# Weight sums held back by marks, attention in whole-chunk steps, and the last norm in blocks: a two-layer hybrid decoder on one core

## The chip, the cores and the metric

The kernel runs on one core of one Trainium2 chip. A core has five engines that run their own instruction queues and wait for each other by semaphores: TensorE (PE; its weight loads are shown as PEld), VectorE (DVE), ScalarE (ACT), GpSimd (POOL) and SyncE (SP). SP, ACT and POOL also issue DMAs, which 16 DMA engines carry out. The metric is the device time of one execution in microseconds (us), the median of several runs. "Line" numbers (L187) are those of the kernel before.

## The reference

Two layers over x of 512 rows by 2048. A layer projects its input to 16 heads in three groups: six forgetting-attention heads ("fox", causal attention with a cumulative log-forget bias), six sparse-attention heads ("dsa", rotary; an indexer with 16 small heads picks 128 keys per query) and four heads that read 256 memory rows. Every head is multiplied by a SiLU gate, all heads go through one output projection, and x becomes LayerNorm(alpha * x + y). All values are float32.

```
h = x @ w_in                       # q, k, v, gate of every group, forget logits, indexer
fox: softmax(q.k * scale + c_q - c_k, causal) @ v,  c = cumsum(log_sigmoid(f_logit + b_forget))
dsa: keys = top_k(sum_h relu(q_idx.k_idx) * w_idx);  softmax(q.k * scale over keys) @ v
mem: softmax(q.k_mem * scale) @ v_mem,  (k_mem, v_mem) = mem @ w_mem_kv
y = concat(fox, dsa, mem) * silu(gates) @ w_out
x = layer_norm(alpha * x + y) * ln_gain + ln_bias
```

## The kernel before

The work is a stream of weight chunks of 1 MB (128 x 2048, `raw`). `load_w` has SP load a chunk two chunks ahead into one of three buffers; `split_w` splits each half of it, three halves ahead of its use, into a high part on ScalarE (`whi`, L180) and the rest on VectorE (`wlo`, L181). `product` makes one float32 product out of three matmuls (L187 to L189). A layer's chunks are, in order: the memory's values (`mv`, 4) and keys (`mk`, 4), the queries and gates of the memory heads (`mq`, `mg`, 4 pairs), one chunk of small columns, eight for the indexer's queries (`iq`), and then for every four heads four chunks of values (`val`) followed by gate, query and key of each head (`fg`, `fq`, `fk` or `dg`, `dq`, `dk`). A chunk of queries is 48 matmuls of 128x512.

The output projection (`out`) is a seven-product matrix scheme, 14 steps of two chunks (`OUT_ORDER`), 24 matmuls of 128x512 a chunk. It needs sums of weight blocks, T1 to T4. `weight_sums` makes them in DRAM: 32 DMAs of 1 MB a layer, all issued by POOL, half of them plain copies (L307) and half adds into memory (L304).

What isn't matmuls of the stream is written as generators. `begin` puts one on a list and `tick` advances each by a step; `tick` runs after the first half of a chunk and at its end, so the order in the code is fixed by hand. `attend` is one fox or dsa head: scores (`s`, L530), softmax (`pr`), transposes of the probabilities (`pt`, L560) and the product with the values (`po`), each of them a step or two after the other. For a fox head `forget_bias` loads a row of forget sums (`ck`, POOL's queue) and lets POOL make the bias tiles (`bt`). `late_operands` splits the left operands of the output projection. The tiles of 128x512 come from one pool of 69 buffers (`slot`), the accumulators from 8 banks (`bank`); a new tile waits until its buffer's last readers are done.

At the end of layer 1 the rows are normalised in four blocks of 128 rows (`finish`). Blocks 2 and 3 are complete after step ("Q5", 1), six chunks before the end; blocks 0 and 1 with the last chunk. `finish` treats the first 512 columns on ScalarE and POOL (L713 to L715, output DMA on ScalarE's queue) and the other three on VectorE in two passes (L718, L721, output DMA on SP's queue).

Of the kernel before, what the change touches and what calls it, by code (L numbers as in the profile page):

```python
# [139 lines left out]
def kernel(  # L140
# [147 lines left out]

    where = {c: i for i, c in enumerate(all_chunks())}

    def weight_sums(l):

        every = [(pair, g) for pair in range(2) for g in range(2)]
        for name, first, second in (("T1", (0, 0), (0, 1)), ("T3", (0, 1), (1, 1)),
                                    ("T2", "T1", (1, 1)), ("T4", "T2", (1, 0))):
            for step in (first, second):
                for pair, g in every:
                    key = (l, name, pair, g)
                    if isinstance(step, str):
                        src = sums[l, step, pair, g]  # L300
                    else:
                        src = wall[where["out", l, 2 * pair + step[1], 2 * step[0] + g]]
                    if step is second:
                        nc.gpsimd.dma_start(sums[key], src, accum_op=ALU.add, max_dma_last_dim=4 * DM)  # L304
                    else:
                        sums[key] = dram.tile([P, DM], F32, name=uid("sum"))
                        nc.gpsimd.dma_start(sums[key], src)  # L307
                    yield 3

    crow_d = [dram.tile([H_FOX, SEQ], F32, name=f"crow{l}") for l in range(DEPTH)]  # L310
    x1_d = dram.tile([SEQ, DM], F32, name="x1")
# [1 line left out]

    active = []

    def begin(gen, wait=0, last=False):
        active.append([wait, gen, last])

    def tick():
        for a in sorted(active, key=lambda a: a[2]):  # L320
            if a[0] > 0:
                a[0] -= 1
                continue
            try:
                a[0] = (next(a[1]) or 1) - 1
            except StopIteration:
                active.remove(a)
# [83 lines left out]
    def small_work(l, sm):  # L411
# [45 lines left out]
        nc.scalar.activation(cq, tp[:, :w], AF.Copy)  # L457
        forget["cq"] = cq

    def forget_bias(l, h):  # L460

        ck = slot("ck")
        nc.gpsimd.dma_start(ck, bass.AP(tensor=crow_d[l].tensor, offset=crow_d[l].offset + h * SEQ,
                                        ap=[[0, P], [1, SEQ]]))
        bt = [slot("bt", w=w) for w in BANK_W]
        for qb in range(4):
            b, off, w = PACK[qb]
            c = qb * H_FOX + h
            nc.gpsimd.tensor_scalar(bt[b][:, off:off + w], ck[:, :w], -1.0,
                                    forget["cq"][:, c:c + 1], op0=ALU.mult, op1=ALU.add)  # L470
            d = bt[b][:, off + w - P:off + w]
            nc.gpsimd.affine_select(out=d, in_=d, compare_op=ALU.is_ge, fill=NEG, base=0,
                                    pattern=[[-1, P]], channel_multiplier=1)
        return bt
# [229 lines left out]
                o = 6 * (2 * dc + e)  # L704
                nc.vector.bn_stats(stats[st][:, o:o + 6], z[st, dc][:, e * 256:(e + 1) * 256])

    def finish(st):
        mv, rs = norm_stats(st)
        nmr = small("nmr", 1)
        nc.vector.tensor_scalar(nmr, mv[:, 0:1], rs, -1.0, op0=ALU.mult, op1=ALU.mult)  # L710
        rest = [z.pop((st, c)) for c in range(4)]
        t = rest.pop(0)
        nc.scalar.activation(t, t, AF.Identity, bias=nmr, scale=rs)  # L713
        nc.gpsimd.tensor_tensor(t, t, rows["g", 0], op=ALU.mult)
        nc.gpsimd.tensor_tensor(t, t, rows["b", 0], op=ALU.add)  # L715
        nc.scalar.dma_start(out[st * P:(st + 1) * P, 0:512], t)
        for c, t in enumerate(rest):
            nc.vector.scalar_tensor_tensor(t, t, mv[:, 0:1], rows["g", c + 1], op0=ALU.subtract,  # L718
                                           op1=ALU.mult)
        for c, t in enumerate(rest):  # L720
            nc.vector.scalar_tensor_tensor(t, t, rs, rows["b", c + 1], op0=ALU.mult, op1=ALU.add)  # L721
            nc.sync.dma_start(out[st * P:(st + 1) * P, (c + 1) * 512:(c + 2) * 512], t)


    out_ps, chains, kept = {}, {}, []
# [8 lines left out]
    for i, (kind, l, j, col, _) in enumerate(chunks):  # L734
# [20 lines left out]
        for h in range(2):  # L755
# [14 lines left out]
            if kind == "out" and late:  # L770
                kept += [(left[aname, 2 * col + h], e, w) for e, w in enumerate(parts[n])]
                for st in range(2 if len(kept) == 8 else 0):
                    if st == 0:
                        groups = [(slice(0, 512), zs[0], False)]
                    else:
                        residual(st, 3, zs[1])
                        groups = [(slice(c, c + 256), bank("z"), True) for c in (0, 256)]
                    for c, ps, fresh in groups:
                        for k, (y, e, w) in enumerate(kept):
                            r = slice(e * 256 + st * P, e * 256 + (st + 1) * P)  # L780
                            product(ps[:, c], tuple(a[:, r] for a in y), tuple(a[:, c] for a in w),
                                    fresh and k == 0, k == 7, not fresh)
                        residual(st, 3, ps[:, c], 1, c, True)
                    finish(st)
            elif kind == "out":
                for st in range(2):
                    for e in range(2):
                        r = slice(e * 256 + st * P, e * 256 + (st + 1) * P)
                        product(zs[st], tuple(a[:, r] for a in left[aname, 2 * col + h]),
                                tuple(a[:, e * 512:(e + 1) * 512] for a in parts[n]),  # L790
                                opens and col == h == e == 0,
                                col == h == e == 1, not opens)
            elif kind == "val":
                for st in range(4):
                    for nn in range(2):
                        k = 4 * col + 2 * h + nn
                        product(out_ps[st], tuple(a[:, st * P:(st + 1) * P] for a in xT[k]),
                                tuple(a[:, nn * 512:(nn + 1) * 512] for a in parts[n]),
                                k == 0, k == KT - 1)
            elif kind == "mv":  # L800
                for m in range(2):
                    for nn in range(2):
                        k = 4 * col + 2 * h + nn
                        c = (k % 2) * 256 + m * P
                        product(out_ps[m], tuple(a[:, c:c + P] for a in memT[k // 2]),
                                tuple(a[:, nn * 512:(nn + 1) * 512] for a in parts[n]),
                                k == 0, k == KT - 1)
            elif kind == "mk":
                for kk in range(8):
                    k = 8 * h + kk  # L810
                    m = memT[k // 2]
                    c = (k % 2) * 256
                    product(ps[:, :256], weight_cols(n, kk), tuple(a[:, c:c + 256] for a in m),
                            k == 0, k == KT - 1)
            else:
                cols = slice(P if kind == "iq" else 0, SEQ)
                for kk in range(8):
                    k = 8 * h + kk
                    product(ps[:, cols], weight_cols(n, kk), tuple(a[:, cols] for a in xT[k]),
                            k == 0, k == KT - 1)  # L820
            del parts[n]
            if h == 0:
                tick()
        if kind == "mk":
            t = slot("kmem", F32R)
            split(ps[:, :256], t[:, 0:256], t[:, 256:512])
# [49 lines left out]
        elif kind == "out" and col == 1 and not late:  # L876
            for t, nb, sign in targets:
                for st in range(2):
                    residual(2 * t + st, 2 * pair + nb, zs[st], sign,
                             last=name in ("P2", "Q4", "Q5", "Q3"))  # L880
            if l == DEPTH - 1 and j == ("Q5", 1):
                finish(2)
                finish(3)
        if kind == "mg":
            begin(mem_head(l, j))
        if kind in ("fk", "dk"):
            begin(attend(l, kind[0], j), 1)

        if kind == "mg" and j == (2 if l == 0 else 0):
            begin(weight_sums(l))  # L890
        if kind == "dg" and j >= 2:
            first_difference(j - 2)
        if kind == "dq" and j == H_DSA - 1:
            begin(early_operands())
        if kind == "out":
            a = 2 * step + col
            if l == DEPTH - 1 and a == 18:
                load_rows(l)
            if l == 0 and 12 <= a < 20:
                load_mem(a - 12)  # L900
            if l == 0 and 20 <= a:
                split_mem(a - 20)
            if a == 27:
                chains.clear()
                terms.clear()
                if l == 0:
                    begin(next_x())
# [67 lines left out]
```

## Time and profile before

| | |
|---|---|
| three runs | 2026.77, 2027.49 (median), 2028.43 us |
| profiled execution | 2027.68 us, its span 2025.9 us |
| TensorE busy | 1978.8 us, 98% of the span, granted clock 0.990 |
| VectorE, ScalarE, POOL busy | 63%, 36%, 11% |
| DMA | 314.07 MB, mean 155 GB/s |

The profile page lists busy times, the span in slices, the DMA queues, the chain that ended last and the costliest groups of instructions. A row of the timeline has start, duration, engine, line, operation, output tile and inputs, and in brackets how long the engine was idle before it and what ended that. Durations in the row of an instruction group are minimum, median and maximum in ns. A busy matmul row is longer than the time to the next one's start, since matmuls are pipelined.

### The profile page before, as it was taken

The page shows a single profiled execution, that of the slowest core. Times are in us where ns is not written, and L with a number is a line of the kernel's source. Part 1 is how long each engine was busy: PE and PEld are TensorE (multiplying, and loading weights), DVE is VectorE, ACT ScalarE, POOL GpSimd, SP SyncE. Part 2 cuts the span into 40 slices and gives each one's busy share as a digit, 9 for nine tenths or more (in the row PEclk, how much of TensorE's full clock was granted, in tenths as well). Part 3 has the DMA queues.
Part 4 walks back from the last instruction along what each step waited for, and adds up shares of the span by engine and source line. Part 5 has one row for each costly group of instructions (what it writes and reads, how often), then busy time and mean ns, then how long its engine had stood idle before and what let it go on. Part 6 is the DMA issues. An engine that isn't in the chain of part 4 may idle for free.

```text
span 2025.9 us, 24094 instructions
## 1 busy us (share of the span) xinstructions
PE 1978.8 (98%) x9506; PEld 1681.2 (83%) x9506; DVE 1273.3 (63%) x1999; ACT 726.4 (36%) x1142; POOL 232.7 (11%) x329
## 2 busy tenths in 40 slices
PE   7999999999999999999999999999999999999985
PEld 6889988888888888788898898888888888887864
DVE  4545755678446356778866476557864544667886
ACT  4433343323323222444473333433222322334432
POOL 0000101311100000100049111021011000001011
PEclk8999999999999999999999999999999999999997
DMA  9422763654362222456556547444545322226543
GB/s 357 163 83 104 202 214 90 198 171 159 121 187 84 93 94 84 146 211 227 184 189 241 154 130 237 140 170 135 166 151 152 104 83 84 85 85 216 203 164 142
DMA packets 48910, 314.07 MB, mean 155 GB/s; under 512 B 6545, under 2 KB 6545, under 8 KB 18589
## 3 DMA queue, kind: packets, MB, share of 16 engines
q1 hardware_dynamic: 36444, 224.43, 30.7%
q0 software_dynamic: 11776, 87.07, 16.0%
q8 instruction: 74, 1.21, 0.2%
q10 hardware_dynamic: 576, 1.05, 0.1%
q14 instruction: 40, 0.32, 0.0%
HBM read 304.10 MB, written 75.52 MB: 187 GB/s over the span
## 4 chain that ended last, share of the span: by engine, by line
PE 92%; DVE 3%; issue 2%; DMA 1%; ACT 1%; SPq 0%; POOL 0%; DVEq 0%; ACTq 0%; POOLq 0%
PE c L187 19%; PE c L189 19%; PE c L188 19%; PE v L189 5%; PE v L187 5%; PE v L188 5%; PE z L188 4%; PE z L189 4%; PE z L187 4%; PE pt L560 1%; DMA raw<-in_wall_dram 1%; PE po L188 1%; PE po L189 1%; PE po L187 1%; PE ix L487 1%
## 5 line engine op out<-in xcount | busy, mean ns | idle before, releaser
L187 PE MATMUL c<-xh,whi 128*128 128x512 f32 (+1 forms) x1696 | 650.0, 383 | 0.0
L189 PE MATMUL c<-xh,wlo 128*128 128x512 f32 (+1 forms) x1696 | 646.9, 381 | 0.1
L188 PE MATMUL c<-xl,whi 128*128 128x512 f32 (+1 forms) x1696 | 646.4, 381 | 0.0
L181 DVE TENSOR_TENSOR wlo<-raw,whi 128x1024 fp32r<-128x1024 f32 (+1 forms) x405 | 502.0, 1244 | 228.8 <-ACT whi L180 227.1
L180 ACT ACTIVATE whi<-raw 128x1024 fp32r<-128x1024 f32 (+1 forms) x405 | 423.4, 1052 | 342.9 <-PE z L189 97.6
L189 PEld LDWEIGHTS c<-xh,wlo 128*128 128x128 f32 x1696 | 318.3, 188 | 57.5 <-DVE wlo L181 0.4
L188 PEld LDWEIGHTS c<-xl,whi 128*128 128x128 f32 x1696 | 318.6, 188 | 54.7
L187 PEld LDWEIGHTS c<-xh,whi 128*128 128x128 f32 x1696 | 318.5, 188 | 54.5
L187 PE MATMUL z<-whi,yh 128*128 128x512 f32 (+1 forms) x450 | 176.2, 391 | 10.4 <-ACT whi L180 10.4
L188 PE MATMUL z<-wlo,yh 128*128 128x512 f32 (+1 forms) x450 | 176.2, 392 | 1.5 <-DVE wlo L181 1.4
L189 PE MATMUL z<-whi,yl 128*128 128x512 f32 (+1 forms) x450 | 175.5, 390 | 0.0
L187 PE MATMUL v<-whi,xh 128*128 128x512 f32 x384 | 150.2, 391 | 0.0
L189 PE MATMUL v<-whi,xl 128*128 128x512 f32 x384 | 149.7, 390 | 0.0
L188 PE MATMUL v<-wlo,xh 128*128 128x512 f32 x384 | 149.5, 389 | 0.0
L187 PEld LDWEIGHTS z<-whi,yh 128*128 128x128 f32 x450 | 85.7, 191 | 28.6 <-ACT whi L180 11.4
L188 PEld LDWEIGHTS z<-wlo,yh 128*128 128x128 f32 x450 | 85.5, 190 | 20.3 <-DVE wlo L181 3.1
L189 PEld LDWEIGHTS z<-whi,yl 128*128 128x128 f32 x450 | 85.6, 190 | 17.4
L497 DVE SCALAR_TENSOR_TENSOR acc<-rel,iw,acc 128x256 f32<-128x256 f32 (+2 forms) x90 | 52.8, 625 | 52.4 <-ACT rel L491 52.4
L189 PEld LDWEIGHTS v<-whi,xl 128*128 128x128 f32 x384 | 72.1, 188 | 15.3
L188 PEld LDWEIGHTS v<-wlo,xh 128*128 128x128 f32 x384 | 72.1, 188 | 14.8
L187 PEld LDWEIGHTS v<-whi,xh 128*128 128x128 f32 x384 | 72.1, 188 | 14.6
L180 ACT ACTIVATE qh<-rope 128x512 fp32r<-128x512 f32 x24 | 15.2, 633 | 185.8 <-DVE rope L402 185.8
(173 smaller groups left out, 2214.0 us busy)
## 6 DMA issues: line engine op xcount, KB each, us to landing
raw<-in_wall_dram SPq DMA_DIRECT2D x167, 1024.0 KB, 4.9
sum<-in_wall_dram POOLq DMA_DIRECT2D x32, 1024.0 KB, 15.0
raw<-sum SPq DMA_DIRECT2D x32, 1024.0 KB, 4.9
memraw<-in_memt_dram SPq DMA_DIRECT2D x16, 256.0 KB, 5.5
xraw<-in_xt_dram SPq DMA_DIRECT2D x16, 256.0 KB, 9.0
z<-in_x_dram POOLq DMA_DIRECT2D x16, 256.0 KB, 4.8
x<-z POOLq DMA_DIRECT2D x16, 256.0 KB, 4.5
z<-x POOLq DMA_DIRECT2D x16, 256.0 KB, 5.8
```

The costliest lines, as they stand in the source:

```text
L180: nc.scalar.activation(hi, src, AF.Copy)
L181: nc.vector.tensor_tensor(lo, src, hi.bitcast(F32), op=ALU.subtract)
L187: nc.tensor.matmul(ps, ah, bh, start=start, stop=False, skip_group_check=more)
L188: nc.tensor.matmul(ps, ah, bl, start=False, stop=False, skip_group_check=more)
L189: nc.tensor.matmul(ps, al, bh, start=False, stop=stop, skip_group_check=more)
L487: nc.tensor.matmul(o, st[:, qb * P:(qb + 1) * P], kl2[:, :w], start=False, stop=True)
L497: nc.vector.scalar_tensor_tensor(a, rel, wq, a, op0=ALU.mult, op1=ALU.add)
L560: nc.tensor.transpose(tp[tb][:, toff + (qb - kt) * P:toff + (qb - kt + 1) * P], pr[b][:, off + kt * P:off + (kt + 1) * P], ident)
```

## The change

Six edits. (1) `weight_sums` begins at the first value chunk of a layer instead of the third (layer 0) or first (layer 1) memory gate, with one DMA a chunk instead of one in one and a half. (2) Each of these DMAs has a mark ahead of it, `pool_waits`: VectorE copies a constant of 128x1, and POOL multiplies it, so that POOL can't go on until VectorE has come to this place. (3) In the output projection `attend` advances only at the end of a chunk. (4) The forget rows are loaded by SP after the `fq` chunk of the head instead of by POOL at its start. (5) `finish` goes column block by column block, ScalarE scales, VectorE multiplies by the gain; for row blocks 2, 3 and 0 the bias is written to the output ahead (`bias_rows`) and the block is added to it in memory by a DMA of POOL; row block 1 adds the bias on VectorE and is written by SP. Blocks 2 and 3 are generators, a column block a step. (6) The earlier part of the last residual of row block 1 is added before them.

```
+    def pool_waits():
+        mark, seen = small("mark", 1), small("seen", 1)
+        nc.vector.tensor_copy(mark, mhalf)
+        nc.gpsimd.tensor_tensor(seen, mark, mhalf, op=ALU.mult)
...
+                    pool_waits()
                     if step is second:
                         nc.gpsimd.dma_start(sums[key], src, accum_op=ALU.add, max_dma_last_dim=4 * DM)
...
-                    yield 3
+                    yield 2
...
-    def tick():
+    def tick(half=False):
         for a in sorted(active, key=lambda a: a[2]):
+            if half and a[3]:
+                continue
...
+    def load_ck(l, h):
+        cks[h] = slot("ck")
+        nc.sync.dma_start(cks[h], bass.AP(tensor=crow_d[l].tensor, offset=crow_d[l].offset + h * SEQ,
+                                          ap=[[0, P], [1, SEQ]]))
...
+    def bias_rows(st):
+        r = out[st * P:(st + 1) * P, :]
+        nc.gpsimd.dma_start(r, bass.AP(tensor=bias.tensor, offset=bias.offset + (DEPTH - 1) * DM,
+                                       ap=[[0, P], [1, DM]]))
...
-    def finish(st):
+    def finish(st, add=True):
         mv, rs = norm_stats(st)
         nmr = small("nmr", 1)
         nc.vector.tensor_scalar(nmr, mv[:, 0:1], rs, -1.0, op0=ALU.mult, op1=ALU.mult)
...
+        for c in range(4):
+            t = z.pop((st, c))
+            o = out[st * P:(st + 1) * P, c * 512:(c + 1) * 512]
+            nc.scalar.activation(t, t, AF.Identity, bias=nmr, scale=rs)
+            nc.vector.tensor_tensor(t, t, rows["g", c], op=ALU.mult)
+            if add:
+                nc.gpsimd.dma_start(o, t, accum_op=ALU.add)
+            else:
+                nc.vector.tensor_tensor(t, t, rows["b", c], op=ALU.add)
+                nc.sync.dma_start(o, t)
+            yield 1
...
-                        residual(st, 3, zs[1])
                         groups = [(slice(c, c + 256), bank("z"), True) for c in (0, 256)]
...
-                    finish(st)
+                    for _ in finish(st, st == 0):
+                        pass
...
-                tick()
+                tick(kind == "out")
...
             if l == DEPTH - 1 and j == ("Q5", 1):
-                finish(2)
-                finish(3)
+                residual(1, 3, zs[1])
+                begin(finish(2))
+                begin(finish(3), 4)
...
-            begin(attend(l, kind[0], j), 1)
-        if kind == "mg" and j == (2 if l == 0 else 0):
+            begin(attend(l, kind[0], j), 1, whole=True)
+        if kind == "val" and j == col == 0:
             begin(weight_sums(l))
+        if kind == "fq":
+            load_ck(l, j)
...
+            if l == DEPTH - 1 and a in (8, 10, 12):
+                bias_rows((2, 3, 0)[(a - 8) // 2])
```

POOL's queue at the start of the program, before; `sum` is a weight sum in DRAM, `rope` the rotary add of an indexer chunk, `crow` the forget sums:

```order
L274 MEMSET mhalf 128x1
L307 DMA sum_1199<-in_wall_dram 16x16384
L307 DMA sum_1313<-in_wall_dram 16x16384
L307 DMA sum_1462<-in_wall_dram 16x16384
L402 TENSOR_TENSOR rope_1557<-rope_1557,rope_1558 128x384
L307 DMA sum_1619<-in_wall_dram 16x16384
```

And after, where the adds of the indexer chunks come first and a mark (`seen`) precedes every sum:

```order
L274 MEMSET mhalf 128x1
L413 TENSOR_TENSOR rope_1551<-rope_1551,rope_1552 128x384
L413 TENSOR_TENSOR rope_1648<-rope_1648,rope_1649 128x384
L459 MEMSET ones_1698 6x512
L461 DMA crow_157<-crow_1699 6x512
L413 TENSOR_TENSOR rope_1731<-rope_1731,rope_1732 128x384
...
L413 TENSOR_TENSOR rope_2103<-rope_2103,rope_2104 128x384
L295 TENSOR_TENSOR seen_2180<-mark_2179,mhalf 128x1
L314 DMA sum_2183<-in_wall_dram 16x16384
```

The first three copies have moved from the very start to behind all eight indexer chunks and a mark.

VectorE where layer 1's output projection starts, before; `pr<-s` are the last dsa head's scores, `rec` and what follows its softmax, `wlo` weight halves:

```order
L181 TENSOR_TENSOR wlo_14679<-raw_14573,whi_14678 128x1024
L181 TENSOR_TENSOR yl_14695<-y_8942,yh_14694 128x512
L537 SCALAR_TENSOR_TENSOR pr_14715<-s_14700,acc_10178 128x512
...
L181 TENSOR_TENSOR wlo_14731<-raw_14676,whi_14730 128x1024
L549 RECIPROCAL rec_14721<-sums_14720 128x4
```

And after, where `z` are the residuals at the end of a step of the projection:

```order
L181 TENSOR_TENSOR wlo_14935<-raw_14829,whi_14934 128x1024
L181 TENSOR_TENSOR yl_14951<-y_9066,yh_14950 128x512
L181 TENSOR_TENSOR wlo_14955<-raw_14932,whi_14954 128x1024
L553 SCALAR_TENSOR_TENSOR pr_14987<-s_14972,acc_10294 128x512
...
L181 TENSOR_TENSOR wlo_15005<-raw_14932,whi_15004 128x1024
L181 TENSOR_TENSOR yl_15021<-y_9458,yh_15020 128x512
L181 TENSOR_TENSOR wlo_15025<-raw_15002,whi_15024 128x1024
L713 SCALAR_TENSOR_TENSOR z_14924<-z_14924,z_14922 128x512
...
L565 RECIPROCAL rec_14993<-sums_14992 128x4
```

A second weight half now stands ahead of the scores, and between scores and softmax two halves and the residuals of a step stand where one half stood.

VectorE after the last residuals of step ("Q5", 1), before; `row` are gain and bias rows:

```order
L710 TENSOR_SCALAR nmr_15712<-mv_15707,rs_15708 128x1
L718 SCALAR_TENSOR_TENSOR z_14923<-z_14923,mv_15707,row_15581 128x512
...
L721 SCALAR_TENSOR_TENSOR z_15015<-z_15015,rs_15728,row_15591 128x512
L181 TENSOR_TENSOR wlo_15750<-raw_15667,whi_15749 128x1024
L181 TENSOR_TENSOR wlo_15766<-raw_15747,whi_15765 128x1024
```

And after:

```order
L732 TENSOR_SCALAR nmr_15972<-mv_15967,rs_15968 128x1
L737 TENSOR_TENSOR z_15355<-z_15355,row_15836 128x512
L181 TENSOR_TENSOR wlo_15980<-raw_15926,whi_15979 128x1024
L737 TENSOR_TENSOR z_15164<-z_15164,row_15840 128x512
L181 TENSOR_TENSOR wlo_15999<-raw_15977,whi_15998 128x1024
L737 TENSOR_TENSOR z_15632<-z_15632,row_15844 128x512
```

Both blocks' twelve passes stood ahead of the next weight half; now one multiply does.

More of the change, by code (lines that the diff above doesn't have):

```diff
@@ L314, with begin @@
     active = []
-    def begin(gen, wait=0, last=False):
-        active.append([wait, gen, last])
-    def tick():
+    def begin(gen, wait=0, last=False, whole=False):
+        active.append([wait, gen, last, whole])
+    def tick(half=False):
         for a in sorted(active, key=lambda a: a[2]):
+            if half and a[3]:
+                continue
             if a[0] > 0:
@@ L458, in small_work @@
         forget["cq"] = cq
+    cks = {}
+    def load_ck(l, h):
+        cks[h] = slot("ck")
+        nc.sync.dma_start(cks[h], bass.AP(tensor=crow_d[l].tensor, offset=crow_d[l].offset + h * SEQ,
+                                          ap=[[0, P], [1, SEQ]]))
     def forget_bias(l, h):
-        ck = slot("ck")
-        nc.gpsimd.dma_start(ck, bass.AP(tensor=crow_d[l].tensor, offset=crow_d[l].offset + h * SEQ,
-                                        ap=[[0, P], [1, SEQ]]))
+        ck = cks.pop(h)
         bt = [slot("bt", w=w) for w in BANK_W]
@@ L710, in finish @@
         nc.vector.tensor_scalar(nmr, mv[:, 0:1], rs, -1.0, op0=ALU.mult, op1=ALU.mult)
[L711 to L722, printed above, removed]
+        for c in range(4):
[9 more added lines that the diff above has]
+            yield 1
     out_ps, chains, kept = {}, {}, []
```

## The prediction

> **What bounds the kernel now.** I read the page first, then stretches of the span, then the rows around each hole in TensorE's work.
>
> ```profile
> span 2025.9 us, 24094 instructions
> PE 1978.8 (98%) x9506; PEld 1681.2 (83%) x9506; DVE 1273.3 (63%) x1999; ACT 726.4 (36%) x1142; POOL 232.7 (11%) x329
> PE 92%; DVE 3%; issue 2%; DMA 1%; ACT 1%; SPq 0%; POOL 0%; DVEq 0%; ACTq 0%; POOLq 0%
> 0.00:50.00 50.00, 39.41 (x203) 33.32 (x204) 24.75 (x29) 23.73 (x32) 2.42 (x10) 0.90 0.97 356
> 1900.00:1950.00 50.00, 49.99 (x221) 41.04 (x220) 42.30 (x58) 23.63 (x28) 4.31 (x8) 1.00 0.71 243
> 1950.00:2000.00 50.00, 38.18 (x148) 29.89 (x147) 36.82 (x51) 14.22 (x15) 7.37 (x6) 0.86 0.35 127
> 2000.00:2050.00 50.00, 8.62 (x61) 7.95 (x59) 17.20 (x27) 1.63 (x2) 7.34 (x6) 0.84 0.12 42
> ```
>
> TensorE is the bound: 98% busy, 92% of the chain that ended last. Only 47 us of the span have no matmul, and nearly all of it is at the two ends. (In rows of stretches: length, busy time and count of PE, PEld, DVE, ACT, POOL; then TensorE's clock, DMA share, GB/s.) The change removes no matmul, so it can only win holes, and the slow clock behind them. A 128x512 matmul takes 50/221 = 0.226 us from start to start. The sum is made against the profiled execution, 2027.68 us with a span of 2025.9; it lies 0.2 us above the median, which I leave out.
>
> **Weight sums held back (head).**
>
> ```profile
> 1.47 1.69 POOL L307 DMA_DIRECT2D sum<-in_wall_dram  x3
> 8.00:10.00 2.00, 0.00 (x0) 0.00 (x0) 0.00 (x0) 0.00 (x0) 0.00 (x0) 0.67 0.89 347
> 10.00:12.00 2.00, 0.00 (x0) 0.00 (x0) 0.00 (x0) 0.00 (x0) 0.00 (x0) 0.50 1.66 557
> 14.98 1.32 ACT L180 ACTIVATE whi<-raw 128x512 fp32r<-128x512 f32 x2 [9.09 <-DMA raw<-in_wall_dram]
> 15.66 0.79 PE L187 MATMUL v<-whi,memh 128*128 128x512 f32 x1 [8.49 <-ACT whi L180]
> 5.90:39.30 33.40, 24.64 (x96) 18.96 (x97) 16.62 (x20) 14.49 (x19) 0.00 (x0) 0.85 0.96 355
> 39.30:62.30 23.00, 23.00 (x193) 22.96 (x193) 19.46 (x25) 16.72 (x26) 0.00 (x0) 1.00 1.00 395
> ```
>
> POOL has nothing ahead of the first three copies of 1 MB, so it issues them at 1.47 us, in the middle of the first weight loads. The second quarter of the first weight chunk then lands 9 us late, while the DMA engines move 347 and 557 GB/s of something else. TensorE idles 8.49 us and restarts at half clock. From 5.9 to 62.3 us it has 96 matmuls of 0.226 and 193 that ran unhindered in 23.0: 21.7 + 23.0 = 44.7 of 56.4 us, so 11.7 us are lost. After the change the copies stand behind the first value chunk, and the quarter follows the first within a few us. ScalarE splits pieces of 128x512 in 0.66 us (1.32 for two), faster than TensorE consumes them, so I leave about 1 us of waits: **-10.6** (bounds: -6, if later pieces are also late, to -11.7). The stretch to 39.3 us shows 355 GB/s; the four value chunks of the memory and their operand are 6 MB, 17 us of that, against 21.7 us of matmuls, so DMA doesn't become the bound.
>
> The 64 marks cost a VectorE copy and a POOL multiply of 128x1 each. The nearest rows:
>
> ```profile
> 2004.83 0.15 DVE L637 TENSOR_SCALAR rs<-mv 128x1 f32<-128x1 f32 x1
> 2005.06 0.55 POOL L638 TENSOR_TENSOR rs<-rs,mhalf 128x1 f32<-128x1 f32 x1 [31.14 <-DVE rs L637]
> L304 POOL DMA_DIRECT2D sum<-in_wall_dram x32: 790/878/1809, 210.1 to 1548.8; - x32
> DMA to landing us min/median/max: 4.7/7.8/28.3
> ```
>
> That is 10 us of VectorE and 35 of POOL over 1.3 ms, beside TensorE's work: 0 (at worst all of VectorE's 10). What queues behind a mark on POOL are a sum's DMA (0.9 us to issue) and the next fox head's bias; VectorE waits for that bias in its score step, half a chunk later, and weight halves are split three halves ahead of their use: 3 x 24 x 0.226 = 16.3 us of cover. The sums now end some 57 chunks into a layer, while the output projection starts at chunk 73. The forget rows move from POOL's queue to SP's, where a row has weight loads behind it. SP runs two chunks ahead of the place at which a row is issued; what a row waits for there is a step of VectorE, TensorE or POOL at most half a chunk later than the one the next weight load waits for anyway: 0 (at worst that half chunk, which the same lead covers).
>
> **Attention by whole chunks (start of the output projection).**
>
> ```profile
> 841.37 0.50 PE L187 MATMUL s<-qh,qh 128*128 128x512 f32 x1 [0.85 <-ACT qh L180]
> 842.10 0.50 PE L188 MATMUL s<-ql,qh 128*128 128x512 f32 x1 [0.22 <-DVE ql L181]
> 851.91 2.40 PE L560 MATMUL pt<-ident,pr 128*128 128x128 f32 x10 [2.40 <-DVE pr L552]
> 851.90:855.50 3.60, 3.59 (x14) 3.31 (x15) 3.15 (x5) 1.75 (x4) 0.54 (x1) 0.54 0.28 61
> 1832.90 0.50 PE L187 MATMUL s<-qh,qh 128*128 128x512 f32 x1 [0.85 <-ACT qh L180]
> 1833.63 0.50 PE L188 MATMUL s<-ql,qh 128*128 128x512 f32 x1 [0.23 <-DVE ql L181]
> 1843.44 1.42 PE L560 MATMUL pt<-ident,pr 128*128 128x128 f32 x10 [2.39 <-DVE pr L552]
> ```
>
> The last DSA head of each layer is squeezed into output chunks half as long as the earlier ones: TensorE waits for its key (0.85 + 0.22) and for its softmax (2.40). In layer 0 the clock also falls to 0.54 for 3.6 us, which is 3.6 x 0.46 = 1.7 us more. With a step per chunk, 24 x 0.226 = 5.4 us lie between steps where 2.7 lay; the late work needs 2.4 us more than it had, so it is ready. **-5.1** in layer 0, **-3.5** in layer 1 (bounds: 0 to -8.6 together). What is late next: the head's output, now after the fifth chunk; its operand is split by the sixth and used at the ninth.
>
> **Norm of row blocks 2 and 3 in steps.**
>
> ```profile
> 1958.23 0.68 DVE L699 TENSOR_TENSOR z<-z,z 128x512 f32<-128x512 f32 x1
> 1962.22 0.21 DVE L710 TENSOR_SCALAR nmr<-mv,rs 128x1 f32<-128x1 f32 x1 [0.69 <-POOL rs L638]
> 1974.40 1.06 ACT L180 ACTIVATE whi<-raw 128x1024 fp32r<-128x1024 f32 x1 [3.73 <-POOL z L715]
> 1975.50 0.29 PEld L187 LDWEIGHTS z<-whi,yh 128*128 128x128 f32 x1 [9.09 <-ACT whi L180]
> 1976.25 10.05 SPq L203 DMA_DIRECT2D raw<-in_wall_dram  x4
> 1982.49 2.00 ACT L180 ACTIVATE whi<-raw 128x1024 fp32r<-128x1024 f32 x2 [7.04 <-DMA raw<-in_wall_dram]
> 1966.80:1988.30 21.50, 9.68 (x22) 6.66 (x22) 13.91 (x18) 6.75 (x8) 3.66 (x3) 0.69 0.73 260
> ```
>
> Both norms now stand in one piece ahead of the next weight split. ScalarE, whose queue holds an output DMA that waits for POOL's two passes, resumes only at 1974.40; SP holds three output DMAs of each block ahead of the next weight loads, which start at 1976.25 and are used at 1982.49. From 1966.8 to 1988.3 us TensorE makes 22 matmuls, 22 x 0.226 = 5.0 us of work, at a mean clock of 0.69. The change takes both kinds of output DMA off ScalarE and SP (they go to POOL as adds into memory) and leaves one block, an activation and a multiply, per half chunk. What is late next is the first step: from the residuals at 1958.23 to the end of the scale's bias at 1962.43 are 4.2 us, then the added residual 0.7, activation 0.8, multiply 0.7 and the split 1.2, 7.6 us against a cover of three half chunks, 8.2 us. It fits narrowly, so **-16.5** (bounds: -6, when only the second norm's half goes, to -16.5).
>
> [...]
>
> **The last row blocks.**
>
> ```profile
> 2005.78 3.10 DVE L718 SCALAR_TENSOR_TENSOR z<-z,mv,row 128x512 f32<-128x512 f32 x3
> 2005.89 0.82 ACT L713 ACTIVATE z<-z,nmr,rs 128x512 f32<-128x512 f32 x1 [10.08 <-DVE nmr L710]
> 2011.80 1.20 DVE L699 TENSOR_TENSOR z<-z,z 128x512 f32<-128x512 f32 x2
> 2015.62 3.08 DVE L718 SCALAR_TENSOR_TENSOR z<-z,mv,row 128x512 f32<-128x512 f32 x3
> 2018.62 3.07 DVE L721 SCALAR_TENSOR_TENSOR z<-z,rs,row 128x512 f32<-128x512 f32 x3
> L402 DVE TENSOR_TENSOR rope<-rope,rope x26: 682/693/693, 176.6 to 1831.5; 128x512 f32<-128x512 f32 x24, 64x512 f32<-64x512 f32 x2
> sum<-in_wall_dram POOLq DMA_DIRECT2D x32, 1024.0 KB, 15.0
> ```
>
> Block 0's norm keeps VectorE from 2005.78 to 2011.80, and only then come block 1's residuals. After: four activations of 0.82 from 2005.89, each followed by a multiply of 0.69, end at 2009.9: 1.9 us earlier, and one residual of 0.6 is gone from there. Block 1 itself: activation 0.9, then eight operations of 0.67 = 6.3 us, where 2015.62 to 2021.69 are 6.1. Net **-2.3** (bounds: -3.5 to +3). Block 0's four adds are issued by 2011 and the whole MB would land by 2026 - 2.3 even at the 15.0 us of a 1 MB sum, about where block 1's last write lands, so 0. The three bias DMAs (3 MB in a burst near 1860 us) could hold a weight load as the sums did, 9 us; a load is issued five half chunks of 12 x 0.226 = 2.7 us ahead of its split and has three more until its use: 0.
>
> **Sum.** -10.6 - 5.1 - 3.5 - 16.5 - 2.3 = -38.0; 2027.68 - 38.0 = **1989.7 us**.
>
> **Rivals.**
> - The head's wait isn't the sums' doing, or loads stay late without them: 2000.3 us. For it: a first load has latency of its own, and the loads alone filled the DMA engines until 62 us. Against: the 9.09 us in which nothing for ScalarE landed while 557 GB/s moved. [...] 12%.
> - A stall stays near the end: the first norm step misses its cover, or the bias burst holds a load: up to +9, 1998.7 us. 14%.
> - Slower: POOL, tied to VectorE by the marks, is held by a sum's add until the fox bias comes too late. An add that holds POOL for the longest landing, 28.3 us, exceeds the cover of 16.3 by 12 us; over twelve fox heads that is +144 - 38: 2134 us. It decides from holds near 16.3 + 38/12 = 19.5 us per head on. Against: the adds now stand four marks, about four chunks, behind their copies. 3%.
> - Several of these in part, between 2001 and 2024: 7%.
>
> **Numbers.** The forecast, 1986 to 1995, has 64%. From 1986 to 2001 I take in the first two rivals and leave out about 12%. A change under 0.2% (4 us) isn't told from none. Faster by more: 95%; within: 2%; slower: 3%.
>
> **What would show it.** Right: no wait of 8 us before 20 us, and TensorE's first 128x512 product of the projections near 52 us instead of 62; no idle before s and pt of the last DSA head; no hole and clock 1.00 from TensorE's start of the output projection to its end; some 15 us from the last matmul to the end instead of 17.3. Wrong: a new releaser ahead of PE rows in the fox heads (bt), SP waiting at a forget row, or the last adds landing after the last plain write.

## The result, and the profile after

The changed kernel takes 1994.31 us (median of 4 runs, 1992.93 to 1996.41) against 2027.95 for the kernel before on the same chip: a ratio of 0.9836, 95% interval 0.9819 to 0.9853, 33.6 us less. The prediction was 1989.7, with 1986 to 1995 as the likeliest range and 1986 to 2001 with its first two rivals. The profiled execution is the slowest of the four, 1996.41 with a span of 1994.6, so its rows add up to 2.1 us more than the median.

The page of the changed kernel, its first lines and the chain:

```profile
span 1994.6 us, 24228 instructions
PE 1972.8 (99%) x9506; PEld 1678.1 (84%) x9506; DVE 1265.4 (63%) x2059; ACT 733.2 (37%) x1154; POOL 237.9 (12%) x388
PE 92%; issue 3%; DVE 3%; ACT 1%; DMA 1%; POOL 0%; SPq 0%; POOLq 0%; ACTq 0%; DVEq 0%
```

TensorE has the same 9506 matmuls and is without work for 22 us instead of 47. What it still waits for, in the view of waits (what waits, for what, us in total, times, longest):

```profile
PE z L188 <- DVE wlo L181: 2.7, 2, 2.1
PE pt L576 <- DVE pr L568: 2.3, 2, 1.1
PE warm L272 <- POOL mhalf L274: 1.4, 1, 1.4
PE v L187 <- ACT whi L180: 1.2, 2, 0.6
```

The waits of 8 us are gone. Three small ones remain besides the wait for the constant of the warm-up at the start (warm), which the kernel before has too: the first weight pieces (v), a softmax in each layer (pt), and one of the last weight splits (z). The head, by stretches, the first product of the projections, and ScalarE's rows with what ended its idle time:

```profile
0.00:12.00 12.00, 9.25 (x34) 6.68 (x34) 3.43 (x6) 5.03 (x7) 0.74 (x7) 1.00 0.78 234
12.00:50.00 38.00, 37.59 (x234) 33.49 (x235) 28.91 (x35) 25.13 (x35) 0.00 (x0) 1.00 1.03 407
54.68 0.40 PE L187 MATMUL c<-xh,whi 128*128 128x512 f32 x1
6.77 1.27 ACT L180 ACTIVATE whi<-raw 128x512 fp32r<-128x512 f32 x2 [1.42 <-DMA raw<-in_wall_dram]
9.44 0.63 ACT L180 ACTIVATE memh<-memraw 128x512 fp32r<-128x512 f32 x1 [1.40 <-DMA memraw<-in_memt_dram]
11.23 0.63 ACT L180 ACTIVATE whi<-raw 128x512 fp32r<-128x512 f32 x1 [1.15 <-DMA raw<-in_wall_dram]
12.67 1.06 ACT L180 ACTIVATE whi<-raw 128x1024 fp32r<-128x1024 f32 x1 [0.81 <-DMA raw<-in_wall_dram]
```

The first projection starts at 54.68 instead of 62.37. ScalarE still waits 0.8 to 1.4 us for each of these rows, whose pieces take 0.6 to 1.1 to split; in the first 12 us the DMA engines move 234 GB/s, afterwards 407. From 12 us on TensorE is nearly never idle.

The end: TensorE's late product, VectorE's rows ahead of it, SP's last weight loads, ScalarE's last splits, and two stretches behind.

```profile
1972.50 0.78 PE L188 MATMUL z<-wlo,yh 128*128 128x512 f32 x1 [2.07 <-DVE wlo L181]
1967.34 1.22 DVE L181 TENSOR_TENSOR wlo<-raw,whi 128x1024 fp32r<-128x1024 f32 x1
1968.47 0.68 DVE L715 TENSOR_TENSOR z<-z,z 128x512 f32<-128x512 f32 x1
1969.19 0.76 DVE L721 BATCH_NORM_STATS2 stats<-z 128x6 f32<-128x256 f32 x2
1969.86 0.67 DVE L715 TENSOR_TENSOR z<-z,z 128x512 f32<-128x512 f32 x1
1970.57 0.75 DVE L721 BATCH_NORM_STATS2 stats<-z 128x6 f32<-128x256 f32 x2
1971.24 1.21 DVE L181 TENSOR_TENSOR wlo<-raw,whi 128x1024 fp32r<-128x1024 f32 x1
1940.42 14.31 SPq L203 DMA_DIRECT2D raw<-in_wall_dram  x3
1966.03 2.00 ACT L180 ACTIVATE whi<-raw 128x1024 fp32r<-128x1024 f32 x2
1974.00:1976.00 2.00, 2.00 (x9) 1.81 (x8) 0.94 (x2) 0.00 (x0) 0.00 (x0) 0.51 0.00 0
1976.00:1978.00 2.00, 2.00 (x19) 2.00 (x18) 1.24 (x5) 0.00 (x0) 0.56 (x1) 1.00 0.00 0
```

SP and ScalarE are early: the last load was issued by 1954.7, and ScalarE's half of the last split ended at 1968.0. VectorE has no pause here, and two residuals with their statistics stand ahead of its half: 1968.47 to 1971.24, 2.8 us. TensorE waits 2.07 of them, and works at half clock from 1972.5 to 1976.0, which costs half of these 3.5 us, about 1.75. The same wait, 2.1 us, stands in the profiles of four runs below (the last norm's part alone, rows late, rows early, no marks). In the first of them the clock fell again: behind it, from 1990.0 to 1992.5 us, matmuls of 128x256 start 0.21 us apart, and 0.12 from 1992.7 on.

### The profile page after: what moved, and what is told of

Its sections match the earlier page's. It is cut to its first block, busy times and chain, and to the rows that moved or that the text cites. A ratio compares the mean times of both kernels' runs of the same rounds, so it can differ in the third digit from the quotient of the medians.

```text
span 1994.6 us, 24228 instructions
## 1 busy us (share of the span) xinstructions
PE 1972.8 (99%) x9506; PEld 1678.1 (84%) x9506; DVE 1265.4 (63%) x2059; ACT 733.2 (37%) x1154; POOL 237.9 (12%) x388
## 4 chain that ended last, share of the span: by engine, by line
PE 92%; issue 3%; DVE 3%; ACT 1%; DMA 1%; POOL 0%; SPq 0%; POOLq 0%; ACTq 0%; DVEq 0%
PE c L187 19%; PE c L189 19%; PE c L188 19%; PE v L189 5%; PE v L187 5%; PE v L188 5%; PE z L188 3%; PE z L187 3%; PE z L189 3%; PE pt L576 1%; PE po L189 1%; PE po L188 1%; PE po L187 1%; DVE wlo L181 1%; PE ix L503 1%
## 5 line engine op out<-in xcount | busy, mean ns | idle before, releaser
L295 POOL TENSOR_TENSOR seen<-mark,mhalf 128x1 f32<-128x1 f32 x64 | 13.4, 210 | 675.4 <-DVE mark L294 563.0
L187 PEld LDWEIGHTS v<-whi,xh 128*128 128x128 f32 x384 | 72.1, 188 | 14.6
```

The costliest lines, as they stand in the source:

```text
L187: nc.tensor.matmul(ps, ah, bh, start=start, stop=False, skip_group_check=more)
L295: nc.gpsimd.tensor_tensor(seen, mark, mhalf, op=ALU.mult)
```

## Experiments

Each run is timed against the kernel before on its own chip (code is cut to the lines that matter, with dots where lines are left out); differences are of medians in one set of runs, or else of what each version gains on its own runs of before (the changed kernel: 33.6).

### The three parts alone

The kernel before with the sums begun at the value chunks, and their marks:

```
-        if kind == "mg" and j == (2 if l == 0 else 0):
+        if kind == "val" and j == col == 0:
             begin(weight_sums(l))
...
+                    pool_waits()
...
-                    yield 3
+                    yield 2
```

> The kernel before with one part of the change alone: the weight sums begin behind the first value chunk of each layer, each held by its mark. Theory (the copies of 1 MB held the first loads, and what is left of the head's wait is the loads' own pace): the first product of the projections moves from 62.37 to about 54.7 us, so 7.7 us are won: 2020. The prediction's own size of this term, 10.6: 2017. Rival (the first loads are late without the copies too, and the changed kernel won its time elsewhere): 2027, no change.

Measured: 2111.85 against 2028.83, ratio 1.0411 (1.0397 to 1.0425), **83 us slower**. Every theory on record missed. The first product does come at 53.59 us, so the head won its time. The loss lies in the fox heads. TensorE's waits, what GpSimd's bias operations (bt) waited for, and one head on GpSimd:

```profile
PE pt L567 <- DVE bt L559: 60.2, 12, 7.8
L476 POOL TENSOR_SCALAR bt<-ck,cq 128x128 f32<-128x128 f32 (+3 forms) x48 | 25.4, 530 | 105.4 <-DMA ck<-crow 105.4
601.13 0.18 POOL L295 TENSOR_TENSOR seen<-mark,mhalf 128x1 f32<-128x1 f32 x1 [12.05 <-DVE mark L294]
601.33 0.54 POOL L314 DMA_DIRECT2D sum<-sum  x1
601.87 0.59 POOL L470 DMA_DIRECT2D ck<-crow  x1
609.20 0.37 POOL L476 TENSOR_SCALAR bt<-ck,cq 128x128 f32<-128x128 f32 x1 [6.75 <-DMA ck<-crow]
DMA to landing us min/median/max: 6.5/10.2/11.8
```

In the order of before, a forget row (ck) is issued by GpSimd right ahead of the bias that uses it. GpSimd used to run ahead, so the row's landing, the time from its issue to the arrival of its data (3.7 us in the median), cost TensorE nothing. A mark makes GpSimd wait for VectorE; the row is issued only when its head is reached, behind a sum of 1 MB, and lands 10.2 us later (median, last line). GpSimd waits 105.4 us over twelve heads, VectorE waits for the bias, TensorE for VectorE, 60.2 us. The rest of the loss goes with a slower clock: 0.973 over this run, 0.992 over the next.

The same without the marks:

> The sums moved as in the run before, but without the marks: nothing but GpSimd's own order holds a copy. Theory (the move alone empties the head; the marks matter afterwards): the first product is near 54.7 us as with marks, but the copies, 32 of them behind each other, are issued in bursts of several MB among the value and forget-head chunks, and weight loads behind them come late: 3 to 9 us given back, 2023 to 2029. Rival (GpSimd's waits at the forget heads' bias space the copies well enough): 2020, the same as with marks.

Measured: 2019.32, ratio 0.9954 (0.994 to 0.9968): 9.5 us won. The first product is at 53.22 us, and no wait of TensorE between the head and the output projection is new. The rival holds, by its time. Its reason fits the trace, where GpSimd waits 51 us for its own earlier copies and longer still at the forget heads, but no run takes these waits away.

The attention by whole chunks alone:

```
+            if half and a[3]:
+                continue
...
-                tick()
+                tick(kind == "out")
...
-            begin(attend(l, kind[0], j), 1)
+            begin(attend(l, kind[0], j), 1, whole=True)
```

> The kernel before with the attention's steps by whole output chunks alone. Theory (read from the changed kernel, where TensorE still waits 1.1 us for pt in each layer since the four residuals stand ahead of the softmax's scaling on VectorE): of 5.2 us of waits and slow clock in layer 0 and 3.5 in layer 1, 1.1 stay in each: -6.4, 2021. The prediction's size, -8.6: 2019. Rival (the work that stands behind is late by as much): within 1 us of before.

Measured: 2021.3, ratio 0.9963 (0.9951 to 0.9976): 7.5 us won. This row of TensorE's waits is what is left:

```profile
PE pt L562 <- DVE pr L554: 2.3, 2, 1.1
```

The last norm's part alone (steps, bias rows, adds in memory):

> The kernel before with the last norm's part alone: blocks 2 and 3 in steps, the bias rows written first and the results of blocks 2, 3 and 0 added in memory, block 1 on VectorE. Theory (the three parts lie in different stretches and add up): what the other two leave of the 33.6 us, -19.5, 2008. The prediction's size of the two terms: -18.8, 2008.7. Rival (part of it was won because the other parts freed GpSimd and the queues): -14 or less, 2013 or more.

Measured: 2011.39, ratio 0.9914 (0.9901 to 0.9928): 17.4 us won. The wait of 2.07 for the last split is there as in the changed kernel. The parts together, leaving the marks out: 9.5 + 7.5 + 17.4 = 34.4, against 33.6 for the whole change. Within the noise they add up.

### The marks and the forget rows

The changed kernel with the rows back in the attention step:

```
-        if kind == "fq":
-            load_ck(l, j)
...
-        ck = cks.pop(h)
+        ck = slot("ck")
+        nc.gpsimd.dma_start(ck, ...)
```

> The changed kernel with the forget rows back in the attention step, issued by GpSimd. Theory (a mark ties GpSimd to VectorE, so a row is issued only when its head's step is reached, right behind a sum of 1 MB, and its landing of 8 to 12 us, which GpSimd's lead used to hide, stands ahead of the bias in each of twelve heads): the loss between the two runs with the moved sums, 2111.9 - 2019.3 = 92.5, comes back: 1994.3 + 92.5 = 2087, with GpSimd waiting some 100 us for the rows. Rival (the loss belongs to the marks in the old order of the attention, and the changed order bears it): 1994 to 2010.

Measured: 2084.18 (before 2026.91), ratio 1.0282 (1.0266 to 1.0299): some 90 us lost against the changed kernel, 2087 was expected. GpSimd's wait for the rows is 107.1 us, and in the fox heads TensorE is busy 42.2 of 50 us at a clock of 0.90:

```profile
PE pt L578 <- DVE bt L570: 60.7, 12, 7.8
450.00:500.00 50.00, 42.21 (x188) 35.23 (x187) 31.82 (x72) 10.86 (x19) 7.20 (x17) 0.90 0.53 151
```

The rows early, but issued by GpSimd:

```
-        nc.sync.dma_start(cks[h], ...)
+        nc.gpsimd.dma_start(cks[h], ...)
```

> The changed kernel with the forget rows at their new, early place, but issued by GpSimd instead of SP. Theory (it is the place in time that counts): a row is issued 1.5 chunks, 8.2 us, ahead of its bias; behind a sum it lands in 10.2 us, so the bias comes some 2 us late where it came 8.8 late, and of those the cover of the score step takes all: 1994, no change. Rival (it is the queue: a row on GpSimd's queue waits behind the sum and behind the marks, wherever it stands): a loss of 20 us or more, 2014 and up.

Measured: 1993.5, ratio 0.9836 (0.9819 to 0.9853): no change from 1994.31. The landing is as long as in the slow kernels, but GpSimd no longer waits for it: its bias operations (bt) were idle 0.2 us in all, where the slow kernels have 105.4 and 107.1.

```profile
DMA to landing us min/median/max: 6.8/10.2/10.6
L485 POOL TENSOR_SCALAR bt<-ck,cq 128x128 f32<-128x128 f32 (+3 forms) x48 | 31.2, 649 | 0.2
```

So the place in time counts, not the queue. The changed kernel without the marks:

```
-                    pool_waits()
```

> The changed kernel without the 64 marks, the sums begun at the same place and the forget rows on SP. Theory (the place at which the sums begin does all; the marks only space copies that nothing waits for): 1994, the same within 2 us; what the three parts won alone, 9.5 + 7.5 + 17.4 = 34.4, already makes up the whole 33.6. Rival (the marks keep bursts of sums off the weight loads and the forget rows off the bursts): 1997 or more.

Measured: 1994.17, ratio 0.9838 (0.9823 to 0.9852): the same. The landing of the sums' adds goes from a median of 8.5 to 18.6 us, and GpSimd waits 50 us for its own earlier copies, at no cost. The marks are worth nothing that was measured here, and would cost 90 us without the earlier rows.

### The end of the kernel

The changed kernel without bias rows and adds; VectorE adds the bias, SP writes every block:

```
-                begin(finish(2))
-                begin(finish(3), 4)
+                begin(finish(2, False))
+                begin(finish(3, False), 4)
...
-                    for _ in finish(st, st == 0):
+                    for _ in finish(st, False):
```

> The changed kernel without the bias rows and without adding in memory: in all of the last norm VectorE adds the bias and SP writes the result, in the same steps. Theory (what won the time near the end are the steps; the adds spare VectorE 0.69 us a block): in blocks 2 and 3 VectorE gets 8 x 0.69 = 5.5 us more, of which those of block 3, 2.8, fall where it has no pause, so the last weight split is 2.8 later, and in block 0's norm 2.8 more stand ahead of block 1's last residual, of which 0.5 more than now are behind TensorE's end: +5, 1999. Rival (the adds keep the DMA engines busy and cost as much as they spare): 1994 or less. Second rival (plain writes on SP stand ahead of weight loads again): 2004 or more.

Measured: 2023.32 (before 2028.84), ratio 0.9975 (0.9965 to 0.9984): it gains 5.5 us on before where the changed kernel gains 33.6, so it is 28 us slower, far beyond the theory's 5 and as the second rival has it. SP's own queue, and ScalarE's waits:

```profile
1950.86 8.17 SPq L742 DMA_DIRECT2D out_dram<-z  x2
1959.13 0.37 SPq L203 DMA_DIRECT2D raw<-in_wall_dram  x1
1961.14 13.23 SPq L742 DMA_DIRECT2D out_dram<-z  x2
1974.48 0.37 SPq L203 DMA_DIRECT2D raw<-in_wall_dram  x1
1965.30 1.06 ACT L180 ACTIVATE whi<-raw 128x1024 fp32r<-128x1024 f32 x1 [6.88 <-DMA raw<-in_wall_dram]
1980.72 1.15 ACT L180 ACTIVATE wh<-raw 128x512 fp32r<-128x512 f32 x2 [6.50 <-DMA raw<-in_wall_dram]
```

A write (L742) waits for its column, and the next weight load (L203) stands behind it: the load at 1974.48 is the one that ScalarE waits for until 1980.72. VectorE, with the added operations on it, isn't short of time: from 1940 to 2000 us it sits idle 21.9 us for ScalarE's splits. In the changed kernel SP has issued its last load by 1954.7. With writes on SP, spreading the norm over the half chunks is worse than leaving it in one piece: without the norm's part the change would stand near 2028.8 - 9.5 - 7.5 = 2011.8, an estimate from the parts run alone. Plain writes on GpSimd's queue were not tried, so whether the adding itself, beside its queue, saves anything is open.

The multiplications of block 3 on GpSimd:

```
-            nc.vector.tensor_tensor(t, t, rows["g", c], op=ALU.mult)
+            (nc.gpsimd if st == 3 else nc.vector).tensor_tensor(t, t, rows["g", c], op=ALU.mult)
```

> The changed kernel with the four multiplications by the gain in block 3's last norm on GpSimd instead of VectorE. Theory (VectorE is without a pause from 1962 to 1972.5 and its last weight split comes 2.07 us late, behind two residuals and their sums): 4 x 0.69 = 2.8 us leave VectorE's queue, so the two waits of 0.59 and 2.07 go, and the slow clock behind the second, some 1.7 us, with them: -4.3, 1990. GpSimd has 1.5 for a product and 0.86 for an add's issue in each half chunk of 2.7 us. Rival (the late split is late by its weight load or by ScalarE, not by VectorE): 1994, the wait stays. Second rival (GpSimd's products run beside VectorE's at the cost of its speed): 1992 or more.

Measured: 1997.58, ratio 0.9855 (0.984 to 0.987): slower than the versions with 1993.5 and 1994.2 in the same set by 3.4 to 4.1 us. VectorE's weight splits from 1957 to 1973 in the changed kernel (first two rows) and in this one, from 1955 to 1975 (mean ns behind the busy time):

```profile
L181 DVE TENSOR_TENSOR wlo<-raw,whi 128x1024 fp32r<-128x1024 f32 x4 | 4.9, 1219 | 0.3 <-ACT whi L180 0.3
L181 DVE TENSOR_TENSOR wl<-raw,wh 128x512 fp32r<-128x512 f32 x2 | 1.3, 687 | 0.0
```

```profile
L181 DVE TENSOR_TENSOR wlo<-raw,whi 128x1024 fp32r<-128x1024 f32 x4 | 6.9, 1741 | 1.8 <-ACT whi L180 1.8
L181 DVE TENSOR_TENSOR wl<-raw,wh 128x512 fp32r<-128x512 f32 x2 | 4.6, 2332 | 0.0
1961.86 4.59 DVE L181 TENSOR_TENSOR wl<-raw,wh 128x512 fp32r<-128x512 f32 x2
1961.79 1.59 POOL L737 TENSOR_TENSOR z<-z,row 128x512 f32<-128x512 f32 x1
1964.29 1.60 POOL L737 TENSOR_TENSOR z<-z,row 128x512 f32<-128x512 f32 x1
```

The second rival holds. Four products left VectorE (2.8 us), and six splits took 4.6 + 6.9 - 1.3 - 4.9 = 5.3 us longer. A split of 0.69 us beside a GpSimd product of 1.59 took 2.3, as long as the two durations one after the other (2.28). Why they add up, no run here shows.

Two orders changed: the last split ahead of the two residuals, and the attention's step ahead of the four residuals of the first product.

```
+            if i == len(chunks) - 3:
+                split_w(2 * len(chunks) - 1)
+            if j == ("P1", 0):
+                tick()
             for t, nb, sign in targets:
...
-        tick()
+        if not (kind == "out" and col == 1 and j == ("P1", 0)):
+            tick()
```

> The changed kernel with two orders changed: the last weight split stands ahead of the two residuals with their statistics on VectorE, and the softmax's scaling of the last head of each layer ahead of the four residuals. Theory (both waits are VectorE's order alone): the wait of 2.07 us and some 1.7 us of slow clock behind it go, and twice 1.1 us for pt: -6.0, 1988.3. Rival (VectorE is short of time there, and what is moved back is late instead: the next product waits for its bank or its operand): 1993 or more.

Measured: 1989.62 (before 2028.84), ratio 0.981 (0.9796 to 0.9823): it gains 39.2 us on before, 5.6 more than the changed kernel (4.7 by the medians alone), near the theory's 6.0, in which 1.7 were for the slow clock of one profiled execution. Both waits are gone; behind the first loads TensorE's list has only these:

```profile
PE z L188 <- DVE wlo L181: 0.6, 1, 0.6
PE c L189 <- DVE wlo L181: 0.3, 1, 0.3
```

The last matmul ends at 1973.5 and the span at 1988.1: a tail of 14.6 us behind it, where the changed kernel has 13.4. Block 0's products now end 1.6 us after TensorE, so 1.2 us went to the tail.

The first weight chunk in two pieces instead of four (`load_w(0, 2)`):

> The changed kernel with the first weight chunk loaded in two pieces of 512 KB, rows of 4 KB, instead of four of 256 KB with rows of 2 KB. The first 12 us move 234 GB/s where the next 38 move 407, at a DMA share of 0.78 and 1.03. Theory (short rows set the pace of the first loads): the chunk is complete earlier and the first product of the projections comes near 52.5 us: -2, 1992. Rival (the pace is set by all the transfers that run at once, whatever their rows): the first piece of twice the size lands about 1 us later and the rest as before, 1994 to 1995.

Measured: 1993.51, ratio 0.9828 (0.9815 to 0.9842), within the noise of 1994.31. The profiles lean to the theory: the first product is at 52.09 us, and at 52.18 in the last version below, which has two pieces too, where six profiles with four pieces and the sums moved (the changed kernel, the sums with and without marks, rows early, no marks, two orders) have 52.78 to 54.68; the first 12 us move 286 GB/s in this run against 234 to 262 in those six. By the first product this is worth about 1 us, which the times can't tell from nothing. Inconclusive.

The two orders and the two pieces together, with block 1's last residuals ahead of the second half of block 0's products:

> The version with the two orders changed, and with two more edits: the first weight chunk in two pieces, and block 1's last residuals and statistics ahead of the second half of block 0's four scaled columns on VectorE. Theory (from the last matmul to the end 14.6 us pass in the version with two orders, since 2.1 us of block 0's products lie between TensorE's last result and the residual of it; half of them go to the gaps in which VectorE waits for GpSimd's power and ScalarE): the tail is about 13.6, so -1.0, and the pieces give at most 0.8: 1988 to 1988.6. Rival (the displaced products delay block 1's bias or its activations by as much): the tail stays at 14.6, 1988.8 to 1989.6.

Measured: 1988.66 (before 2027.42), ratio 0.9807 (0.9793 to 0.982): the lowest time, 38.8 us under its before, but not told apart from the version with two orders, 39.2 under its own. Its tail is 1971.8 to 1985.7, 13.9 us, nearer the theory's 13.6 than the rival's 14.6; the time lies between the two and decides nothing.

## Why the prediction was right, point by point

- **Head, -10.6.** Right in mechanism: with the copies moved, the wait of 8.49 is gone, and the time alone shows -9.5. The step mis-sized is "I leave about 1 us of waits": the first product came at 54.68, not 52. TensorE's first product is at 5.4 us; with 44.7 us of matmuls it would be at 50.1, so 4.6 us are still lost in the profiled run: TensorE is idle for 1.8 of them, and the rest lies in matmuls that start further apart (2.7 are lost in the best profile of the same head, 52.78). DMA was taken as no bound from 355 GB/s, a mean to 39 us; the first 12 us have 234. Moving nothing but the copies gave the time, so it was they that held the loads: from 4 to 8 us of the run before, GpSimd's queue moved 1.44 MB in 28 packets and SP's 0.32 MB in 182, some 51 and 1.8 KB each. In what order the packets went, no run here shows.
- **Marks, 0.** Right as a number, by luck of the pair. The prediction listed what queues behind a mark on GpSimd in the new order, where the forget rows are no longer there, and then priced the rows' move as a cost only. The runs price the two edits apart: marks without the move +92.5 (2111.85 - 2019.32), with it 0; the early rows alone are worth nothing without marks to cure. The third rival, at 3%, had the right place, bias late in the fox heads, with its cause as a sum's add; the cause was the landing of a 256 KB row behind a sum.
- **Forget rows past SP, 0.** Right. SP does wait at them, which the prediction had named as a sign of being wrong:

```profile
SPq L475 <- DVE acc L513: 86.4, 4, 26.8
```

  but TensorE waits for no weights in the fox heads; the lead of two chunks covers it. As a sign it was badly chosen.
- **Attention, -8.6.** Measured -7.5. "The late work needs 2.4 us more than it had, so it is ready" left out that the softmax's scaling stands behind the four residuals on VectorE. 2.3 us stayed, as the row of the run alone shows; with that order undone they went.
- **Blocks 2 and 3 in steps, -16.5, and the last blocks, -2.3.** Together -18.8, measured -17.4. The first was too large: the step "it fits narrowly" held for block 2's chain, but VectorE had no room for block 3's products, two residuals and the last split, and 0.59 + 2.07 of waits stayed, in this execution with some 1.75 of slow clock. The second was too small, by more than its bounds of -3.5 to +3 allow: the tail is 3.9 us shorter (4.8 in the run of this part alone), which leaves some 13 of the 17.4 to the first. From the last matmul (1981.2) to the end are 13.4 us, not 15; before they were 17.3:

```profile
1978.87 2.81 DVE L737 TENSOR_TENSOR z<-z,row 128x512 f32<-128x512 f32 x4 [0.88 <-ACT z L736]
1981.60 0.42 DVE L715 TENSOR_TENSOR z<-z,z 128x256 f32<-128x256 f32 x1
```

  Block 0's four products are done 0.4 us after TensorE, and block 1's residual follows; before, that was 3.2 us late (2011.80 against 2008.62).
- **Slow clock.** Half clock (0.51) lasted from 1972.5 to 1976.0 behind the one hole left, 3.5 us. Whether a hole drops the clock is another matter, and the prediction priced the slow clock of one profiled execution as if every one had it. In the run with block 3's products on GpSimd, TensorE waited 2.04 us until 1969.50, and its matmuls behind that start 0.23 us apart; it waited 2.01 us until 1974.53, and they start 0.43 apart. Of the two holes before pt in the kernel before, 2.40 us dropped the clock (0.54 behind it) and 2.39 did not (1.00 from 1843.4 to 1847.0).
- **Rivals.** "The head's wait isn't the sums' doing" is refuted by the run with the sums moved alone. "A stall stays near the end" came true in part: 0.59 + 2.07 us of its price of 9, and 1.75 more where the clock fell. The bias rows, issued from 1838.9 to 1840.0 us, held no load that was waited for: TensorE has no gap behind them.

```profile
1850.00:1900.00 50.00, 50.00 (x225) 41.51 (x224) 39.99 (x52) 24.16 (x30) 2.72 (x5) 1.00 0.69 253
```

By the parts run alone the terms were 1.1 (head), 1.1 (attention) and 1.4 us (norm) too large, 3.6 together; the parts add up to 0.8 more than the whole. That makes 4.4 of the 4.6 us by which the time came out above 1989.7; the rest lies between the profiled execution of before, 2027.68, and the median here, 2027.95. The account is not as sharp as it looks: the medians of the kernel before alone differ by up to 2 us between sets of runs, 2026.91 to 2028.84.

## What to carry to other kernels

A wait added to an engine's queue must be priced with all that the queue issues behind it, and above all its DMAs: what used to be issued early by an engine that ran ahead is issued late from then on, and its whole landing comes to light (here 10.2 us a row in the median, twelve times, in a loss of 92.5 us). When a change holds such a wait and a moved load together, price each without the other. And output writes that wait for late results belong on a queue with no load behind them; by the waits in the trace that decided most of the 28 us here, and not the operations that came with them, though no run has the one without the other.

## What the runs showed of the hardware that I had not expected

Moving products to an idle GpSimd made the kernel slower: a VectorE split of 0.69 us took 2.3 beside them (the run above).

A hole of 2.07 us in TensorE's work dropped its clock to half for 3.5 us in the changed kernel's profile; in one execution of the run with block 3's products on GpSimd, a hole of 2.04 us did not and one of 2.01, some 5 us later, did. Over the four executions of the changed kernel the mean clock is 0.996 to 0.998. One profile's slow clock is therefore no fixed part of a kernel's time.

Adding in memory was dear for the DMA engines here. The queues from 1976 to 1995 us in the changed kernel (packets, MB, share of 16 engines' time), GpSimd's adds and SP's plain writes, with the median us to landing:

```profile
q0 software_dynamic: 576, 1.05, 38.9%
q1 hardware_dynamic: 576, 1.05, 14.4%
out_dram<-z POOLq DMA_DIRECT2D x4, 256.0 KB, 6.4
out_dram<-z SPq DMA_DIRECT2D x4, 256.0 KB, 2.3
```

The same megabyte took 2.7 times the engines' time. It was the adding and not GpSimd's queue: GpSimd's plain writes of tiles of the same shape (`x`, layer 0, 1060 to 1103 us) took 17.2% of the engines' time for 2.88 MB, 2.6 us of all 16 engines a MB, as SP's writes above do, where the adds took 7.0. The cost is hidden here: from 1976 us on no load is left to wait, and the last two loads, issued among the adds of block 2, landed in 8.6 us against a median of 5.1 without ScalarE waiting for them.
